# Eight broadcast copies issued behind the first RWKV spill of the second block instead of in the first block

## The chip, the cores and the metric

The kernel runs on one core of a Trainium2 chip. The metric is the device time of one execution in microseconds (us). A profiled execution gives a trace with a time for each instruction of the five engines: TensorE (PE; PEld is its weight load), VectorE (DVE), ScalarE (ACT), GpSimd (POOL) and SyncE (SP), which here only issues DMAs.

## The reference

One inference step of a layer of a diffusion backbone, over 256 context and 2,048 latent tokens (64 columns wide), width 1,024. Cut to what matters:

```
h      = rmsnorm(x) * (1 + scale) + shift          # modulation from c and c_ctx
u      = h @ w_in                                  # one input projection
att    = 8 heads: latent tokens attend 8 x 16 neighbours and all context keys,
         score = q k / 8 + rpb[head, row offset, column offset]
rwkv   = 8 heads of RWKV-7 in two directions: kr, r, v (after a width-3 convolution),
         decay and a from two loras, then a scan over the tokens
x      = x + gate * (concat(att, rwkv) @ w_out)
x      = x + gate * ffn(modulated rmsnorm(x))      # gated, width-3 convolution
```

`rpb` holds the learned offsets of the neighbourhood attention. The attention stage reads them from a table in DRAM, `d_rep`, in which each head's 23 rows of 128 values stand 16 times.

## The kernel before, in words

The stages run one after the other: `stage_in` (0 to about 1,180 us), the neighbourhood attention, the scan, the output projection, the FFN. The change lies in `stage_in` (L538).

*Column tiles.* The input projection is worked in 3 blocks `b` of 768 tokens. For each block, 12 tiles of 128 attention columns are computed first, b = 0, 1, 2; then `rwkv_columns` (L808) computes the RWKV columns of b = 2, 1, 0: three lora tiles and four pairs `p` of heads, each pair as three tiles `kr`, `r`, `v`. A tile is one `gemm`: 48 matmuls (L55), three passes (high and low parts of both factors) over 8 slices of the depth. Its weights are loaded two tiles ahead by DMAs that ACT issues (`Weights`, L79) and split by ACT and POOL (L36, L46). The modulated input `h` of block 0 is made in place and spilled to `d_hhi` (SP, L615) and `d_hlo` (ACT, L616); the other blocks load it back.

*Side work of the attention tiles.* `background(f)` runs after each of the 36 attention tiles and takes steps from the generators in the list `side`: `modulate` twice (8 steps and a first one that loads `x` by DMAs on ACT, computes its scale on ACT, L125 and L126, and scales it on DVE, L577; the transposes are L595), then one entry that calls `replicate`, then `rwkv_constants` (its transpose is L771) and `ada_rest` (the other modulation columns; transposes L240, sums L232). Two steps are taken if two or three entries are left, or if one is left and f is even; one step otherwise.

*The copies.* `replicate` (L737) issues eight DMAs on SP (L741). Each writes `d_rep[h]`, 23 x 16 x 128 values, from `rpb[h]` by a broadcast. They are held by `issue_after(W.last.ins)`, where `W.last` is the newest weight load, an instruction of ACT.

*Work behind the RWKV tiles.* `rest(b, p)` is a generator that turns `kr`, `r`, `v` of a pair into the scan's inputs; it is stepped inside the matmuls of the next pair's tiles (8 times a tile). It computes `kk` (L844), the two gates, transposes `v` and spills it to `d_v` (SP, L864), and then for each direction n = 0, 1 writes `ar` (DVE L897 and POOL L898) and `bk` (DVE L893, L896) and stores both (SP, L900). `ar` and `bk` have one buffer each. The results of a tile leave PSUM through `conv3` (ACT L114, DVE L116).

*Order.* Instructions of an engine run in its own order; a scheduler makes these orders from the program's text and dependences when the kernel is built. DMAs of SP and ACT signal through a common set of eight completion semaphores (DMAHW0 to DMAHW7), and a DMA waits until the last one with the same semaphore is done.

Of the kernel before, what the change touches and what calls it, by code (L numbers as in the profile page):

```python
# [33 lines left out]
def copy(eng, dst, src, scale=None):  # L34
    if hasattr(eng, "activation"):
        eng.activation(dst, src, AF.Copy, scale=1.0 if scale is None else scale)  # L36
    elif scale is None:
        eng.tensor_copy(dst, src)
    else:
        eng.tensor_scalar_mul(dst, src, scale)  # L40
# [8 lines left out]
def gemm3(nc, ps, halves, w, h, tick=None):  # L49


    for c in range(KT):
        for n, (A, B) in enumerate(((w[0], h[0]), (w[1], h[0]), (w[0], h[1]))):
            for q, (a, e) in enumerate(halves):
                nc.tensor.matmul(  # L55
                    ps[q][:, : e - a], A[:, c, :], B[c][:, a:e], start=c == 0 and n == 0, stop=c == KT - 1 and n == 2
                )
        if tick:
            tick()
# [61 lines left out]
def rms_scale(nc, pool, x, eps, name):  # L121

    junk = pool.tile([128, D], F32, name=name + "j", tag="rmsj", bufs=1)
    s = pool.tile([128, 2], F32, name=name + "s", tag="rmss", bufs=4)
    nc.scalar.activation(junk, x, AF.Square, accum_out=s[:, 0:1])  # L125
    nc.scalar.activation(s[:, 1:2], s[:, 0:1], AF.Sqrt, bias=eps, scale=1.0 / D)  # L126
    nc.vector.reciprocal(s[:, 0:1], s[:, 1:2])
    return s[:, 0:1]
# [17 lines left out]
def xrows(xp, xs, t):  # L146

    return xp[t * 128 : t * 128 + 128, :] if t < 2 else xs[(t - 2) * 128 : (t - 1) * 128, :]
# [384 lines left out]
def pair_cols(base, p):  # L533

    return ((base + p * 64, 64), (base + 256 + p * 64, 64))


def stage_in(tc, keep, ident, eps, I, P, C, d, R, new_k, new_v):  # L538

    nc = tc.nc  # L540
    wv = I["w_in"][0].rearrange("(c p) f -> p c f", p=128)
    hv = [d[n].rearrange("(c p) n -> p c n", p=128) for n in ("hhi", "hlo")]
    tiles = [((f * 128, 128),) for f in range(12)] * 3
    for b in range(3):
        tiles += [((3072 + i * 128, 128),) for i in range(3)]
        for p in range(4):
            tiles += [pair_cols(1536 + o, p) for o in (512, 0, 1024)]
    with tc.tile_pool(name="k1", bufs=1) as k1, tc.tile_pool(name="g2", bufs=2) as gp, tc.tile_pool(
        name="gps", bufs=2, space=PSUM
    ) as gps:  # L550

        def window(b, cols=(0, WIN)):
            h = [[], []]
            for c in range(KT):
                for x in range(2):
                    t = gp.tile([128, WIN], F32R, name=f"h{x}", bufs=9)
                    if cols:
                        a, e = cols
                        nc.scalar.dma_start(t[:, a:e].bitcast(F32), hv[x][:, c, STARTS[b] + a : STARTS[b] + e])
                    h[x].append(t)  # L560
            return h

        def gemm(h, halves, tick=None):
            ps = [gps.tile([128, 512], F32, name=f"g{q}") for q in range(2)]
            gemm3(nc, ps, halves, W.next(), h, tick)
            W.fetch()
            return ps

        with tc.tile_pool(name="q2", bufs=2) as q2, tc.tile_pool(name="qp", bufs=3, space=PSUM) as qp:
            def load(tiles):  # L570

                out = []
                for j, t in enumerate(tiles):
                    x = q2.tile([128, D], F32, name="x", bufs=8)
                    nc.scalar.dma_start(x, xrows(I["x_prompt"][0], I["x_sample"][0], t))
                    r = rms_scale(nc, q2, x, eps, f"r{j}")
                    nc.vector.tensor_scalar_mul(x, x, r)  # L577
                    out.append(x)
                return out

            def modulate(groups, h=None):


                xs = [load(g) for g in groups]
                yield
                i = 0
                for c in range(KT):
                    rows = slice(c * 128, c * 128 + 128)
                    for g, x in zip(groups, xs):
                        n = len(g) * 128  # L590
                        tok = slice(g[0] * 128, g[0] * 128 + n)
                        m = int(g[0] >= 2)
                        p = qp.tile([128, 512], F32, name="mtp")[:, :n]
                        for j, t in enumerate(x):
                            nc.tensor.transpose(p[:, j * 128 : j * 128 + 128], t[:, rows], ident)  # L595
                        t = q2.tile([128, n], F32, name="mt", tag="zz", bufs=9)
                        if h:
                            hi, lo = h[0][c][:, tok], h[1][c][:, tok]
                        else:
                            hi = q2.tile([128, n], F32R, name="mhi", tag="zz", bufs=9)  # L600
                            lo = q2.tile([128, n], F32R, name="mlo", tag="zz", bufs=9)
                        mc, ac = mul[:, m, c : c + 1], add[:, m, c : c + 1]
                        if i % 3 == 2:
                            nc.vector.tensor_scalar(t, p, mc, ac, op0=ALU.mult, op1=ALU.add)
                            copy(nc.scalar, hi, t)
                        else:
                            nc.scalar.activation(t, p, AF.Identity, scale=mc, bias=ac)
                            copy(nc.vector, hi, t)
                        (nc.vector if h or i % 3 == 0 else nc.gpsimd).tensor_sub(lo, t, hi)
                        i += 1  # L610
                        if not h:
                            nc.sync.dma_start(d["hhi"][rows, tok], hi.bitcast(F32))
                            nc.scalar.dma_start(d["hlo"][rows, tok], lo.bitcast(F32))
                    if h:
                        nc.sync.dma_start(d["hhi"][rows, 0:BLK], h[0][c][:, :BLK].bitcast(F32))  # L615
                        nc.scalar.dma_start(d["hlo"][rows, 0:BLK], h[1][c][:, :BLK].bitcast(F32))  # L616
                    yield

            h = window(0, None)
            first = modulate(GROUPS[:2], h)  # L620
            cond, ones, mul, add = ada_first(
                tc, keep, gp, q2, qp, ident, I["c"][0], I["c_ctx"], I["w_ada"][0], I["b_ada"][0], I["norm1"][0]
            )
            for _ in first:
                pass
            W = Weights(nc, gp, wv, tiles)
            side = [modulate(GROUPS[2:4]), modulate(GROUPS[4:])]
            consts = {}
            side.append(iter(lambda: replicate(tc, C["rpb"], d["rep"], W) or "end", "end"))
            side.append(rwkv_constants(tc, k1, q2, qp, ident, P, consts, W))  # L630
            side.append(ada_rest(tc, q2, qp, cond, ones, I["w_ada"][0], I["b_ada"][0], d["rows"], W))

            def background(f):
                for _ in range(2 if len(side) in (2, 3) or len(side) == 1 and f % 2 == 0 else 1):
                    if side and next(side[0], "end") == "end":
                        side.pop(0)

            for b in range(3):
                if b:
                    h = window(b, ((1, 1 + BLK), (0, WIN))[b - 1])  # L640
                for f in range(12):
                    attention_columns(nc, q2, qp, ident, gemm(h, ((b, b + 384), (b + 384, b + 768))), b, f, d, new_k, new_v)
                    background(f)
            while side:
                background(0)
        rwkv_columns(tc, ident, consts, R, h, window, gemm)


def query_parts(b):
# [84 lines left out]
        tp_out(z, new_v)  # L734


def replicate(tc, rpb, rep, W):  # L737

    with tc.issue_after(W.last.ins):
        for h in range(8):  # L740
            tc.nc.sync.dma_start(rep[h], rpb[h][:, None, :].to_broadcast([23, 16, 128]))  # L741

# [62 lines left out]
    out.update(col=col, wts=wts, lw=lw, bones=bones, tiny=tiny, cmask=cmask)  # L805


def rwkv_columns(tc, ident, consts, R, h, window, gemm):  # L808


    nc = tc.nc
    with tc.tile_pool(name="i1", bufs=1) as i1, tc.tile_pool(name="i2", bufs=2) as i2, tc.tile_pool(
# [15 lines left out]
        def rest(b, p, kr, r, v, lora):  # L828
# [29 lines left out]
            for t in range(0, 6, 3):  # L858
# [2 lines left out]
                    nc.tensor.transpose(tp[:, j * 128 : j * 128 + 128], v[:, (t + j) * 128 : (t + j) * 128 + 128], ident)  # L861
                nc.scalar.activation(vt[:, t : t + 3, :], tp[:, :384].rearrange("p (t d) -> p t d", t=3), AF.Copy)
                yield
            nc.sync.dma_start(  # L864
                R["v"].rearrange("(t p) f -> p t f", p=128)[:, b * 6 : b * 6 + 6, p * 128 : p * 128 + 128], vt
            )
            ms = []
            for n in range(2):
                sg, a = lr[2 * n : 2 * n + 2]
# [68 lines left out]
        for b in (2, 1, 0):  # L938
            if b < 2:
                h = window(b)  # L940
# [633 lines left out]
```

## Time and profile before

| | |
|---|---|
| device time, median of 3 runs | 4527.84 us (4527.21 to 4528.01) |
| the profiled execution: device time | 4528.56 us |
| its span from first to last instruction | 4526.8 us |
| granted TensorE clock, mean over the span | 0.932 of full speed (2.4 GHz) |
| PE / DVE / POOL / ACT busy, share of the span | 85% / 69% / 51% / 41% |
| `d_rep` copies | 8, issued between 30.4 and 122.1 us |
| first read of `d_rep` | 1213.5 us |

Times below are counted from the start of the span. A row of a timeline gives start, duration, engine, line of the kernel, what is written and read, and, in brackets, how long the engine stood idle before it and what ended that. "SPq" and "ACTq" are DMA issues on these engines; the duration there is the issue alone or, for several in one row, to the end of the last.

### The profile page before, as it was taken

To read this page: it belongs to the slowest core of one execution; us is meant where nothing else is said; L and a number is where in the kernel's file an instruction comes from. 1 tells how busy PE (TensorE), PEld (TensorE's weight loads), DVE (VectorE), ACT (ScalarE), POOL (GpSimd) and SP (SyncE) were. 2 spreads that over 40 slices of the span, in tenths; PEclk is the share of its full clock that TensorE was granted. 3 is DMA by queue.
4 is the path that set the end of the run, shared out by engine and by line. 5 is a ranking of instruction groups with operands and counts; after the bars stand their busy time and mean duration, and the time that the engine had idled before them with its cause. 6 is when DMAs were issued, how large, how long until landed. Compare 5 with 4: busy or idle time off the path is not lost. (4 is left out here: it accounts for less than half of the span.)

```text
span 4526.8 us, 78134 instructions
## 1 busy us (share of the span) xinstructions
PE 3852.0 (85%) x29954; PEld 3414.9 (75%) x29954; DVE 3115.0 (69%) x4658; ACT 1845.9 (41%) x3728; POOL 2323.6 (51%) x1879
## 2 busy tenths in 40 slices
PE   6798987888388887899886886999988999889996
PEld 6787877777266666788775665888877999779995
DVE  4325586868577774566664224888888888878887
ACT  2421254544377773455442223333334333343332
POOL 0334344545234336555664444666656776667662
PEclk9899998989599997999998997999988999999998
DMA  5787545453756623323343443221223222232222
GB/s 211 243 280 212 145 117 165 114 159 112 178 116 135 128 58 102 86 76 81 95 102 105 167 149 94 61 66 61 66 80 112 68 64 70 84 106 63 70 70 66
DMA packets 682387, 513.24 MB, mean 113 GB/s; under 512 B 234691, under 2 KB 612612, under 8 KB 677916
## 3 DMA queue, kind: packets, MB, share of 16 engines
q1 hardware_dynamic: 508444, 378.64, 30.0%
q10 hardware_dynamic: 170080, 118.06, 8.8%
q0 software_dynamic: 3488, 11.54, 0.8%
q8 instruction: 236, 3.87, 0.4%
q14 instruction: 139, 1.14, 0.1%
HBM read 369.85 MB, written 139.76 MB: 113 GB/s over the span
## 5 line engine op out<-in xcount | busy, mean ns | idle before, releaser
L46 POOL TENSOR_TENSOR wl<-wr,wh 128x512 fp32r<-128x512 f32 (+1 forms) x349 | 613.2, 1758 | 575.3 <-ACT wh L36 503.8
L55 PE MATMUL g<-h,wh 128*128 128x384 f32 (+1 forms) x2592 | 641.8, 359 | 32.3 <-DVE r L116 8.4
L36 ACT ACTIVATE wh<-wr 128x512 fp32r<-128x512 f32 (+1 forms) x485 | 336.3, 704 | 500.2 <-DMA wr<-in_w_ffn_dram 210.1
L55 PEld LDWEIGHTS g<-h,wh 128*128 128x128 f32 x2592 | 487.6, 200 | 67.1 <-issue 27.7
L507 DVE TENSOR_TENSOR yacc<-yacc,yp 128x512 f32<-128x512 f32 x756 | 479.3, 680 | 28.9 <-PE yp L499 5.2
L456 PE MATMUL u<-hT,wh 128*128 128x386 f32 x1056 | 366.8, 347 | 38.3 <-DVE st L465 24.8
L456 PE MATMUL u<-lT,wh 128*128 128x386 f32 x1056 | 364.4, 345 | 12.2 <-DVE lT L46 12.2
L456 PE MATMUL u<-hT,wl 128*128 128x386 f32 x1056 | 364.4, 345 | 3.8 <-POOL wl L46 3.8
L55 PE MATMUL g<-h,wl 128*128 128x384 f32 (+1 forms) x1296 | 359.9, 355 | 0.0
L499 PE MATMUL yp<-w2h,gh 128*128 128x512 f32 x792 | 273.1, 418 | 48.6 <-DVE yacc L507 20.0
L46 DVE TENSOR_TENSOR wl<-wr,wh 128x512 fp32r<-128x512 f32 (+1 forms) x136 | 251.9, 1853 | 63.2 <-ACT wh L36 63.1
L456 PE MATMUL u<-h,wh 128*128 128x386 f32 x792 | 272.7, 344 | 19.3 <-ACT h L36 17.5
L456 PE MATMUL u<-l,wh 128*128 128x386 f32 x792 | 271.7, 345 | 8.2 <-DVE l L46 7.9
L456 PE MATMUL u<-h,wl 128*128 128x386 f32 x792 | 274.4, 346 | 0.0
L499 PE MATMUL yp<-w2l,gh 128*128 128x512 f32 x792 | 257.8, 404 | 0.0
L499 PE MATMUL yp<-w2h,gl 128*128 128x512 f32 x792 | 257.0, 403 | 0.0
L55 PEld LDWEIGHTS g<-h,wl 128*128 128x128 f32 x1296 | 250.8, 200 | 2.8 <-issue 2.5
L456 PEld LDWEIGHTS u<-hT,wh 128*128 128x128 f32 x1056 | 203.0, 192 | 51.8 <-DVE st L465 31.9
L499 PEld LDWEIGHTS yp<-w2h,gh 128*128 128x128 f32 x792 | 151.6, 193 | 108.9 <-DVE yacc L507 50.1
L354 POOL TENSOR_TENSOR s<-wr 128x512 f32<-128x512 f32 x66 | 85.8, 1300 | 271.3 <-DMA wr<-in_w_ffn_dram 271.3
L456 PEld LDWEIGHTS u<-lT,wh 128*128 128x128 f32 x1056 | 203.4, 193 | 17.8 <-DVE lT L46 17.5
L1273 DVE TENSOR_TENSOR X<-iv,mmask 128x256 f16<-128x256 f32 x360 | 146.3, 422 | 98.7 <-PE iv L1270 93.8
(333 smaller groups left out, 10085.3 us busy)
## 6 DMA issues: line engine op xcount, KB each, us to landing
wr<-in_w_ffn_dram SPq DMA_DIRECT2D x198, 512.0 KB
wr<-in_w_in_dram ACTq DMA_DIRECT2D x45, 512.0 KB
wr<-in_w_in_dram ACTq DMA_DIRECT2D x72, 256.0 KB
d_ar<-ar SPq DMA_DIRECT2D x24, 768.0 KB
d_bk<-bk SPq DMA_DIRECT2D x24, 768.0 KB
kd<-d_ks SPq DMA_DIRECT2D x32, 576.0 KB
bk<-d_bk SPq DMA_DIRECT2D x72, 256.0 KB
ar<-d_ar SPq DMA_DIRECT2D x288, 64.0 KB
```

The lines of the kernel that those rows point to most:

```text
L36: eng.activation(dst, src, AF.Copy, scale=1.0 if scale is None else scale)
L46: lo_eng.tensor_sub(lo, src, hi)
L55: nc.tensor.matmul(ps[q][:, : e - a], A[:, c, :], B[c][:, a:e], start=c == 0 and n == 0, stop=c == KT - 1 and n == 2)
L354: nc.gpsimd.tensor_sub(s3, a11, a21)
L456: nc.tensor.matmul(acc[q], A[a][x][:, c, :], T[t][c][y], start=i < 3 and c == 0 and n == 0, stop=c == KH - 1 and n == 2, skip_group_check= ...
L499: nc.tensor.matmul(yps[q], A[:, t * 128 : t * 128 + 128], B[:, q * 512 : q * 512 + 512], start=n == 0, stop=n == 2)
L507: nc.vector.tensor_add(d, d, yps[q])
L1273: nc.vector.tensor_mul(half(X1, n), X, mk)
```

## The change

`replicate` is no longer an entry of `side`. It is handed to `rwkv_columns`, which calls it once, in `rest`, behind the `d_v` spill of block b=1, pair p=0, and `issue_after` now names that spill. `side` thus begins with four entries, not five.

```diff
@@ stage_in
             consts = {}
-            side.append(iter(lambda: replicate(tc, C["rpb"], d["rep"], W) or "end", "end"))
             side.append(rwkv_constants(tc, k1, q2, qp, ident, P, consts, W))
...
-        rwkv_columns(tc, ident, consts, R, h, window, gemm)
+        rwkv_columns(tc, ident, consts, R, h, window, gemm, lambda at: replicate(tc, C["rpb"], d["rep"], at))
@@ replicate
-def replicate(tc, rpb, rep, W):
+def replicate(tc, rpb, rep, at):
-    with tc.issue_after(W.last.ins):
+    with tc.issue_after(at.ins):
         for h in range(8):
             tc.nc.sync.dma_start(rep[h], rpb[h][:, None, :].to_broadcast([23, 16, 128]))
@@ rwkv_columns, rest
-            nc.sync.dma_start(
+            at = nc.sync.dma_start(
                 R["v"].rearrange("(t p) f -> p t f", p=128)[:, b * 6 : b * 6 + 6, p * 128 : p * 128 + 128], vt
             )
+            if b == 1 and p == 0:
+                behind(at)
```

SP's queue at the start, before (`wb`, `wa` are the modulation's weights, `h_...` the slices of the first block's `h`):

```order
L176 DMA wb<-in_w_ada_dram 128x1024
L741 DMA d_rep<-in_rpb_dram 368x1x128 x3
L615 DMA d_hhi<-h_98 128x768
L615 DMA d_hhi<-h_100 128x768
L741 DMA d_rep<-in_rpb_dram 368x1x128
L615 DMA d_hhi<-h_102 128x768
L615 DMA d_hhi<-h_104 128x768
L741 DMA d_rep<-in_rpb_dram 368x1x128
L615 DMA d_hhi<-h_106 128x768
L615 DMA d_hhi<-h_108 128x768
```

The same place after the change:

```order
L176 DMA wb<-in_w_ada_dram 128x1024
L237 DMA arow<-in_b_ada_dram 1x512
L615 DMA d_hhi<-h_98 128x768
L615 DMA d_hhi<-h_100 128x768
L615 DMA d_hhi<-h_102 128x768
L615 DMA d_hhi<-h_104 128x768
L615 DMA d_hhi<-h_106 128x768
L615 DMA d_hhi<-h_108 128x768
```

The copies are gone from between the spills, and one load of `ada_rest` has come to the front.

SP's queue in `rest` of b=1, p=0, after the change (before, `d_ar` followed the `d_v` spill directly; lines of the changed kernel, one to three off those before):

```order
L901 DMA d_bk<-bk 128x12x128
L863 DMA d_v<-vt 128x6x128
L740 DMA d_rep<-in_rpb_dram 368x1x128 x8
L901 DMA d_ar<-ar 128x12x128
L901 DMA d_bk<-bk 128x12x128
L922 DMA d_g_73<-m_6369 64x768
L901 DMA d_ar<-ar 128x12x128
```

All eight copies stand in a row between that pair's `d_v` spill and its first store of `ar`.

DVE between the two writes of `ar` of that pair, before: n=0 is the first row, n=1 the last.

```order
L897 TENSOR_TENSOR ar<-kk,e_4084 128x12x64
L883 SCALAR_TENSOR_TENSOR t_6314<-zones,w_6210 128x768
L876 TENSOR_TENSOR sl<-m_6282,m_6284 128x768
L877 TENSOR_TENSOR sq<-sq,sl 128x768
L893 SCALAR_TENSOR_TENSOR bk<-a_6234,e_6317 128x12x64
L896 TENSOR_TENSOR bk<-t_6324,e_6317 128x12x64
L116 SCALAR_TENSOR_TENSOR r<-g_6201,cols,r 128x386
L116 SCALAR_TENSOR_TENSOR r<-g_6202,cols,r 128x382
L897 TENSOR_TENSOR ar<-kk,e_4085 128x12x64
```

After the change, the end of that stretch:

```order
L116 SCALAR_TENSOR_TENSOR kr<-g_6446,cols,kr 128x384
L854 TENSOR_SCALAR w_6553<-w_6553 128x768
L854 TENSOR_SCALAR a_6577<-a_6577 128x768
L898 TENSOR_TENSOR ar<-kk,e_4077 128x12x64
L843 SCALAR_TENSOR_TENSOR kk<-kr,cols,sq 128x768
L875 SCALAR_TENSOR_TENSOR sq<-r,cols,kr 128x768
L116 SCALAR_TENSOR_TENSOR r<-g_6544,cols,r 128x386
```

The write for n=1 (`e_4077`) now stands 27 rows behind that for n=0, just ahead of the next pair's `kk` and of the evacuation of `r` of the third pair.

## Rows read from the trace of the kernel before

**Rows 1.** Part 1 of the page: for each engine busy us, its share of the span, and the number of instructions, over the whole span.
```profile
PE 3852.0 (85%) x29954; PEld 3414.9 (75%) x29954; DVE 3115.0 (69%) x4658; ACT 1845.9 (41%) x3728; POOL 2323.6 (51%) x1879
```

**Rows 2.** The table by stretches of time: from:to in us, the stretch's length, then busy us of PE, PEld, DVE, ACT and POOL (xinstructions), the granted TensorE clock, the share of the DMA engines and GB/s.
```profile
40.00:80.00 40.00, 31.93 (x157) 28.59 (x157) 18.58 (x41) 9.89 (x17) 5.21 (x2) 0.99 0.37 131
80.00:120.00 40.00, 19.77 (x77) 18.57 (x77) 5.42 (x8) 5.82 (x13) 1.80 (x1) 0.71 0.43 146
120.00:160.00 40.00, 28.14 (x141) 26.60 (x142) 17.57 (x23) 17.20 (x35) 20.49 (x12) 0.80 0.74 224
160.00:200.00 40.00, 38.88 (x232) 37.52 (x231) 12.69 (x22) 16.98 (x37) 15.81 (x10) 0.99 0.91 279
850.00:900.00 50.00, 42.11 (x208) 37.16 (x207) 40.78 (x36) 25.49 (x38) 28.05 (x14) 0.93 0.45 132
```

**Rows 3.** The instructions that write or read the offset rows `d_rep` (times in the issuing queue: min/median/max ns, first to last start in us).
```profile
L1086 SPq DMA_DIRECT2D raw<-d_rep x64: 302/303/1035, 1213.5 to 1617.2; - x64
L741 SPq DMA_DIRECT2D d_rep<-in_rpb_dram x8: 626/656/10110, 30.4 to 122.1; - x8
```

**Rows 4.** The DMA view of the stretch 44 to 50 us (the packets and rate in it, and what was issued in it), in which only copies of `d_rep` are in flight.
```profile
DMA packets 256, 0.13 MB, mean 22 GB/s; under 512 B 1, under 2 KB 256, under 8 KB 256
...
d_rep<-in_rpb_dram SPq DMA_DIRECT2D x1, 184.0 KB
```

**Rows 5.** Timeline of the SP queue at the start: start us, duration, line, what is issued, count (an entry with a count above 1 runs to the end of its last).
```profile
30.36 19.80 SPq L741 DMA_DIRECT2D d_rep<-in_rpb_dram  x3
...
62.91 14.31 SPq L615 DMA_DIRECT2D d_hhi<-h  x2
...
91.06 15.60 SPq L615 DMA_DIRECT2D d_hhi<-h  x1
```

**Rows 6.** Timeline of ACT in the same stretch; in brackets the idle time before the instruction and what ended it.
```profile
66.91 0.42 ACT L36 ACTIVATE h<-mt 128x256 fp32r<-128x256 f32 x1 [5.63 <-DMA d_rep<-in_rpb_dram]
...
92.84 0.94 ACT L688 ACTIVATE zq<-g 128x256 f32<-128x256 f32 x3 [9.47 <-DMA d_rep<-in_rpb_dram]
...
120.52 0.29 ACT L126 ACTIVATE r2s<-r2s,eps 128x1 f32<-128x1 f32 x1 [18.68 <-DMA d_qs<-zh]
```

**Rows 7.** Timeline of PE, 82 to 141 us: start, duration, line, out<-in, shapes, count, and in brackets the idle time before it and what ended it.
```profile
82.85 1.01 PE L55 MATMUL g<-h,wh 128*128 128x384 f32 x2 [7.52 <-DVE h L38]
...
85.25 1.48 PE L55 MATMUL g<-h,wh 128*128 128x384 f32 x4
...
89.08 0.87 PE L55 MATMUL g<-h,wh 128*128 128x384 f32 x4
...
93.45 0.83 PE L55 MATMUL g<-h,wh 128*128 128x384 f32 x2 [2.80 <-ACT zq L688]
...
96.86 0.48 PE L595 MATMUL mtp<-ident,x 128*128 128x128 f32 x1 [2.41 <-DVE x L577]
...
121.85 0.48 PE L595 MATMUL mtp<-ident,x 128*128 128x128 f32 x1 [14.03 <-DVE x L577]
123.22 1.12 PE L595 MATMUL mtp<-ident,x 128*128 128x128 f32 x4 [0.89 <-DVE x L577]
127.25 0.47 PE L595 MATMUL mtp<-ident,x 128*128 128x128 f32 x1 [2.91 <-DVE x L577]
...
140.48 0.90 PE L595 MATMUL mtp<-ident,x 128*128 128x128 f32 x3 [2.47 <-DVE mt L604]
```

**Rows 8.** Waits of PE from 128 to 560 us: line, what it waited for, us in all, times, longest.
```profile
PE mtp L240 <- DVE acc L232: 12.9, 6, 3.5
PE aux L771 <- DMA h<-d_hlo: 10.3, 1, 10.3
...
PE g L55 <- DMA h<-d_hlo: 3.2, 2, 2.4
```

**Rows 9.** Timeline of the SP queue in the second block (b=1) of the RWKV columns.
```profile
807.11 0.36 SPq L864 DMA_DIRECT2D d_v<-vt  x1
807.58 0.48 SPq L900 DMA_DIRECT2D d_ar<-ar  x1
...
859.25 0.37 SPq L900 DMA_DIRECT2D d_ar<-ar  x1
```

**Rows 10.** Timeline of ACT there: the first and the last of eight weight loads that ACT issues between these two times (814.02, 819.48, 822.23, 829.93, 840.07, 846.41, 851.12 and 865.67).
```profile
814.02 0.38 ACTq L79 DMA_DIRECT2D wr<-in_w_in_dram  x1
...
865.67 0.37 ACTq L79 DMA_DIRECT2D wr<-in_w_in_dram  x1
```

**Rows 11.** Part 6 of the page (DMA issues): what, queue, count, KB each.
```profile
wr<-in_w_in_dram ACTq DMA_DIRECT2D x72, 256.0 KB
d_ar<-ar SPq DMA_DIRECT2D x24, 768.0 KB
```

**Rows 12.** Timeline of DVE there.
```profile
847.91 0.53 DVE L855 TENSOR_SCALAR a<-a 128x768 f32<-128x768 f32 x1
...
861.63 1.64 DVE L116 SCALAR_TENSOR_TENSOR r<-g,cols,r 128x386 f32<-128x386 f32 x3
863.57 2.90 DVE L897 TENSOR_TENSOR ar<-kk,e 128x768 f32<-128x768 f32 x1 [0.30 <-DMA d_ar<-ar]
```

**Rows 13.** Timeline of PE there.
```profile
863.32 0.44 PE L55 MATMUL g<-h,wh 128*128 128x386 f32 x1 [0.76 <-DVE r L116]
869.02 1.01 PE L823 MATMUL lr<-sl,bones 128*128 128x384 f32 x2 [5.26 <-DVE sl L46]
```

More of the change, by code (lines that the diff above doesn't have):

```diff
@@ L805, in rwkv_constants, with rwkv_columns @@
     out.update(col=col, wts=wts, lw=lw, bones=bones, tiny=tiny, cmask=cmask)
-def rwkv_columns(tc, ident, consts, R, h, window, gemm):
+def rwkv_columns(tc, ident, consts, R, h, window, gemm, behind):
     nc = tc.nc
```

## The prediction

> **What bounds the kernel now.** First the share of each engine: TensorE (PE) is busy 85% of the span [rows 1], so an idle stretch of PE is what a change can remove or add. Then the table by stretches [rows 2]: PE works 31.93 of 40 us from 40 to 80, but only 19.77 from 80 to 120 and 28.14 from 120 to 160, with the granted clock at 0.71 and 0.80, and 38.88 from 160 to 200 at 0.99. So the start has a hole. Third, who owns that hole: the copies `d_rep` are issued there, between 30.4 and 122.1 us, though the first reader (L1086) comes at 1213.5 [rows 3]. Fourth, what such a copy costs: with only these in flight, 256 packets of 512 B pass in 6 us, 22 GB/s [rows 4], so 23.4 ns a packet. A copy of 184 KB is 368 packets, 8.6 us; eight are 69 us, one after another even when three are queued.
>
> **How they stop PE now.** SP's queue stands at the spills of `h` for 14.31 and 15.60 us with a copy in between [rows 5]. ACT, which issues DMAs as well and in order, stands still 5.63 and 9.47 us for a copy and 18.68 us for a transfer queued among them [rows 6]. ACT also issues the loads of `x` and computes their scale, so PE waits for `x`: [rows 7] give, between 82.85 and 127.25, waits of 7.52, 2.80, 2.41, 14.03, 0.89 and 2.91, together 30.6 us.
>
> **The change, part by part.**
>
> *Start.* The eight copies leave the head of SP's queue; nothing takes their place but one `arow` load, which comes earlier. The 30.6 us go. With them goes the slow clock after each long wait: four matmuls take 1.48 us at 85.25 but 0.87 at 89.08, when PE has been at work again for 6 us [rows 7]: 0.15 us each. Between 82.85 and 89.08 some 19 matmuls fit at that pace, and as many follow the waits at 93.45 and 96.86: 5 us. What is late next is the modulation chain itself, which is at work when no copy is in the way: one wait like that at 140.48, 2.47 us [rows 7]. Gain 30.6 + 5 − 2.5 = **33 us**. Its ends: if only ACT's and `h`'s waits go and the four waits for `x` stay (2.41 + 14.03 + 0.89 + 2.91 = 20.2), 13 us; if nothing replaces the waits, 36 us. I take 33, because the waits for `x` end with ACT instructions that themselves stood behind the copies [rows 6].
>
> *Pacing of the side work.* The list `side` has four entries in place of five, so the rule "two steps when two or three are left" sets in one entry earlier: the last group of modulations runs two steps a tile instead of one, constants and the `ada` columns come some five to eight tiles earlier. No work is added. PE's waits around it now are 12.9 us for `ada`, 10.3 us at the constants' transpose and 3.2 us for `h` at a block's start [rows 8]. All the `ada` waits gone would be −13; another wait like that of the constants +10. Modulation's spills come in about half the time while the DMA engines are already at 0.91 [rows 2]; I charge one more set of `h` waits, **+3 us**.
>
> *New place.* All eight copies now stand in SP's queue right behind the `d_v` spill of the second block's first pair, issued at T = 807.11 [rows 9]. Nobody waits for them. But the next thing on SP is the store of `ar` for n=0, ready at 807.58 [rows 9]. `ar` has one buffer, so DVE's and POOL's writes of `ar` for n=1 wait for that store to land. Its share on the engine that the copies occupy lies behind all of them. When does it land? About 2 us until the first copy moves; 69 us of copies; weight loads that ACT issues meanwhile, 8 of them [rows 10] of 256 KB [rows 11], which is 1,024 pieces of 256 B, 64 to an engine if spread over 16: 512 packets at between half of and the full 23.4 ns, 6 to 12 us, taken as 9; and the store itself, 4.3 us from its issue at 859.25 [rows 9] to the write that it releases at 863.57 [rows 12]. T + 84, or 891.
>
> DVE works in order. The changed order puts 27 rows of DVE between its two writes of `ar`; the last of them ran before at 847.91 [rows 12], so DVE stops only near T + 41. Behind that write stand the next pair's `kk`, a product, and the evacuation of `r` of the third pair (L116), which before ran at 861.63 [rows 12]. PE's next column tile needs that PSUM buffer: it started at 863.32, T + 56 [rows 13]. After the change: T + 84, then 2.9 us for the write [rows 12], about 2 for `kk` and the product, 1.64 for the evacuation [rows 12]: T + 90.5. PE loses 34 us. A little of PE's other waits there (5.26 at 869.02 [rows 13]) may fall inside; but DVE is busy 40.78 of 50 us in this stretch [rows 2], so its backlog keeps PE from catching up. **+33 us.** Ends: if the store passes the copies and only ACT's semaphores hold (ACT's load of 865.67, T + 58.6 [rows 10], waits for the last copy, T + 71), about +12; if the weight loads take full packet times and PE also gives up the slow clock after a long wait, 34 + 3 + 5 = +42.
>
> A rule to weigh here: the Trainium skill, "DMA: Bandwidth & Descriptors", section "Specifications", gives about 27 GiB/s an engine. An estimate from that page: 188,416 B take 6.5 us, eight 52 us, the new stall is 17 us shorter and the sum is −14 in place of +3. The trace has 22 GB/s and 8.6 us, and the measurement decides.
>
> *Everything later* (attention, scan, output, FFN) keeps its order on every engine; `d_rep` is ready at about T + 80 = 890, 320 us ahead of its reader [rows 3]. Cost 0; cover is that distance.
>
> **Sum.** −33 + 3 + 33 = +3 us on the profiled 4528.56, 4531.6; the runs' median, 4527.84, lies 0.7 lower: **4531 us**. About 0.2% (9 us) is what a measurement of this kernel can tell from no change; +3 is inside it.
>
> **The rivals.**
>
> *A. The copies are hidden at the new place (chance 0.16).* If they ran beside the `ar` store on other engines, or DVE had enough other work, only −33 + 3 is left: 4498 us, faster. For it: PE's work there is not DMA-bound (share 0.45 [rows 2]). Against it: the 22 GB/s of [rows 4] with three queued, and the single `ar` buffer. With only the +12 end: 4510, also faster. The Trainium skill, "DMA: Bandwidth & Descriptors", section "Why a DMA increments its semaphore by 16 and not by 1", speaks against A: a DMA runs on the largest number up to 16 that divides the slowest dimension of both sides, on the lowest-numbered engines; 23 and 368 leave one engine, the same for all eight. By that rule, with which 22 GB/s in [rows 4] agrees, A would need the store to skip that engine.
>
> *B. The waits for `x` stay (chance 0.2).* The start is bound by the loads of `x` and the scale of them, whatever SP does: 20.2 us of the 33 are not won, and the new place costs in full: 4531 + 20 = 4551, slower. It decides as soon as more than 6 us of those 20.2 stay (3 + 6 is over 9). For it: ACT's wait that is the longest, 18.68, is put down to `d_qs`, not to a copy [rows 6]. Against it: that transfer was issued among the copies, and ACT's turn waits on completions shared with SP.
>
> *C. The new pacing decides (chance 0.1).* Crowded spills delay the second block's `h` or the constants by another 10.3 [rows 8]: 4542; or the `ada` waits go: 4515.
>
> **How the numbers follow.** The forecast, with its sizes a little off either way, has 0.54; within it some seven tenths fall inside 0.2% (0.39), 0.11 above and 0.04 below, since the late stall can grow by 9 and the start gain by 3 only. A 0.16 (faster), B 0.2 (slower), C 0.1 (split). Faster 0.25, same 0.39, slower 0.36. The likeliest case alone runs from 4518 to 4543. The range, 4508 to 4554, takes in B, C, and A's partly hidden end of 4510; left out are A's full gain and a late stall at its upper end together with B.
>
> **What would show it.** In the profile after: (1) no `d_rep` before 800; PE's waits for `x` near 100 to 127 gone, PE over 34 of 40 us from 80 to 120, granted clock above 0.9; PE's work of 127.25 done near 95. (2) One run of eight copies from about 775 (T moves by the gain), and 70 to 85 us at some 22 GB/s. (3) The first `ar` write that waits on `DMA d_ar` with 35 to 45 us idle on DVE, and PE idle about 34 us before a column tile, released by DVE `r`. (4) Past it, spans equal to before. I am wrong if (3) shows less than 20 us, or (1) leaves more than 6 us of waits for `x`.

## The result: slower by a third of a percent

| | before | after |
|---|---|---|
| median of 6 runs | 4527.52 us | 4542.85 us (4535.17 to 4546.35) |
| ratio, with 95% interval | | 1.0033 (1.002 to 1.0047) |
| the profiled execution | 4528.56 us, span 4526.8 | 4537.57 us, span 4535.8 |

The change costs 15 us by the medians (9 between the two profiled executions, of which the one after is among the fastest). That is outside the 0.2% that the prediction called no change, and inside its range of 4508 to 4554.

**The hole at the start is gone.** The table by stretches of the changed kernel answers [rows 2] (columns as there):

```profile
40.00:80.00 40.00, 37.04 (x193) 34.35 (x194) 23.05 (x47) 14.58 (x27) 7.07 (x3) 1.00 0.58 216
80.00:120.00 40.00, 33.75 (x186) 32.51 (x186) 19.03 (x25) 18.45 (x38) 21.19 (x12) 0.94 0.82 251
120.00:160.00 40.00, 39.92 (x236) 38.51 (x235) 12.68 (x22) 18.06 (x41) 15.75 (x11) 0.98 0.90 282
850.00:900.00 50.00, 22.13 (x93) 19.59 (x94) 34.59 (x31) 18.05 (x25) 25.70 (x11) 0.67 0.60 174
```

PE works 37.04, 33.75 and 39.92 us where it worked 31.93, 19.77 and 28.14, and the clock of 80 to 120 us is 0.94 in place of 0.71. A new hole stands at 850 to 900: 22.13 us of 50, against 42.11. The copies stand in one row ahead of it, from 778.6 us on, and the first reader comes 7.3 us later than in [rows 3]:

```profile
L1087 SPq DMA_DIRECT2D raw<-d_rep x64: 302/303/1242, 1220.8 to 1626.3; - x64
L740 SPq DMA_DIRECT2D d_rep<-in_rpb_dram x8: 733/9166/10417, 778.6 to 837.2; - x8
```

Of the waits for `x` that [rows 7] show, one is left in PE's timeline between 60 and 135 us:

```profile
89.92 0.33 PE L595 MATMUL mtp<-ident,x 128*128 128x128 f32 x1 [2.26 <-DVE x L577]
```

**How much was won, and how much was lost on the way to the new place.** Two stretches of equal work, cut at the starts of the 1st, 11th and 42nd column tile (a tile is 48 matmuls of L55); first the kernel before, then the changed one:

```profile
56.40:204.80 148.40, 110.08 (x574) 104.79 (x575) 48.09 (x80) 47.95 (x101) 39.12 (x23) 0.86 0.67 213
204.80:551.00 346.20, 309.26 (x1643) 284.18 (x1642) 164.43 (x245) 91.62 (x166) 125.61 (x57) 0.96 0.73 223
```

```profile
56.20:163.40 107.20, 100.85 (x575) 97.68 (x575) 48.62 (x80) 48.16 (x101) 39.23 (x23) 0.97 0.88 285
163.40:521.70 358.30, 316.79 (x1643) 284.79 (x1642) 173.84 (x245) 92.29 (x166) 118.75 (x57) 0.95 0.69 215
```

The first stretch takes 107.2 us in place of 148.4, 41.2 less: PE's time without work falls from 38.3 to 6.4 us (32), and the same 574 or 575 matmuls are busy 9.2 us less, at a clock of 0.97 in place of 0.86. The second stretch takes 358.3 in place of 346.2, **12.1 more**: 4.6 more without work, 7.5 more busy time for the same 1643 matmuls at a slightly lower clock (0.95, before 0.96). So more than half of what the new pace costs is not a wait but longer busy time. PE's waits there, against [rows 8]:

```profile
PE mtp L240 <- DVE acc L232: 9.9, 5, 5.1
PE aux L722 <- ACT zh L718: 6.8, 4, 3.4
PE g L55 <- DMA h<-d_hlo: 4.9, 4, 1.9
PE g L55 <- DMA h<-d_hhi: 3.9, 4, 1.5
PE g L55 <- DVE zl L694: 3.6, 2, 2.4
PE aux L770 <- DMA zh<-in_w_ts_dram: 3.5, 1, 3.5
```

The constants' wait shrank from 10.3 to 3.5 and that for the `ada` sums from 12.9 to 9.9, but `h` (4.9 and 3.9, before 3.2 and 1.9), the attention columns' high and low parts (5.8, before 1.0) and the parts that the transposes of L722 read (9.6, before 7.5) are waited for more.

**The new place.** SP's queue of the changed kernel, which answers [rows 9]; T is the `d_v` spill's issue:

```profile
778.15 0.37 SPq L863 DMA_DIRECT2D d_v<-vt  x1
778.57 67.18 SPq L740 DMA_DIRECT2D d_rep<-in_rpb_dram  x8
845.86 8.49 SPq L901 DMA_DIRECT2D d_ar<-ar  x1
```

T comes 29.0 us earlier than before (807.11). The eight copies hold SP for 67.18 us, and the store of `ar` behind them, ready at T, is issued only at 845.86; its own issue takes 8.49 us, where it took 0.48. DVE, ACT, POOL and PE, in this order (against [rows 12, 13]):

```profile
816.48 0.63 DVE L854 TENSOR_SCALAR a<-a 128x768 f32<-128x768 f32 x1 [3.40 <-ACT a L852]
859.73 0.96 DVE L898 TENSOR_TENSOR ar<-kk,e 128x768 f32<-128x768 f32 x1 [42.62 <-DMA d_ar<-ar]
860.72 2.31 DVE L843 SCALAR_TENSOR_TENSOR kk<-kr,cols,sq 128x768 f32<-128x768 f32 x1
...
864.00 2.18 DVE L116 SCALAR_TENSOR_TENSOR r<-g,cols,r 128x386 f32<-128x386 f32 x4
```

```profile
862.25 1.05 ACT L114 ACTIVATE r<-g,cols 128x385 f32<-128x385 f32 x2 [42.55 <-POOL ar L899]
```

```profile
859.84 2.38 POOL L899 TENSOR_TENSOR ar<-r,e 128x768 f32<-128x768 f32 x1 [43.15 <-DMA d_ar<-ar]
```

```profile
865.80 1.18 PE L55 MATMUL g<-h,wh 128*128 128x386 f32 x2 [36.36 <-DVE r L116]
...
881.75 0.69 PE L822 MATMUL lr<-sh,bones 128*128 128x384 f32 x1 [9.85 <-ACT sh L36]
...
886.26 1.01 PE L822 MATMUL lr<-sl,bones 128*128 128x384 f32 x2 [2.22 <-DVE sl L46]
```

The store lands at about 859.7, T + 81.6. DVE stood 42.62 us before its second write of `ar`, POOL 43.15, and ACT 42.55 behind POOL's half of `ar`: POOL reads `r` of the first pair there, and the third pair's evacuation on ACT (L114) takes that buffer. PE waits 36.36 us for that evacuation, and 9.85 and 2.22 more for the backlog. From the 61st to the 65th column tile's start the changed kernel falls back by 38.7 us (from 29.6 ahead to 9.1 behind); before, then changed:

```profile
824.70:884.90 60.20, 52.04 (x254) 44.82 (x252) 48.19 (x42) 31.45 (x46) 25.66 (x12) 0.94 0.44 124
```

```profile
795.10:894.00 98.90, 50.48 (x243) 44.54 (x242) 44.58 (x41) 26.73 (x39) 28.30 (x13) 0.74 0.38 106
```

PE's time without work rises from 8.2 to 48.4 us; its busy time doesn't grow.

### The profile page after: what moved, and what is told of

The parts are those of the page before. It is cut to its first block, busy times and chain, and to the rows that moved or that the text cites. A ratio compares the mean times of both kernels' runs of the same rounds, so it can differ in the third digit from the quotient of the medians.

```text
span 4535.8 us, 78126 instructions
## 1 busy us (share of the span) xinstructions
PE 3848.6 (85%) x29954; PEld 3405.7 (75%) x29954; DVE 3124.3 (69%) x4658; ACT 1847.0 (41%) x3728; POOL 2317.3 (51%) x1879
## 5 line engine op out<-in xcount | busy, mean ns | idle before, releaser
L55 PE MATMUL g<-h,wh 128*128 128x384 f32 (+1 forms) x2592 | 638.1, 357 | 66.4 <-DVE r L116 42.8
L55 PEld LDWEIGHTS g<-h,wh 128*128 128x128 f32 x2592 | 484.7, 199 | 104.8 <-issue 65.9
L507 DVE TENSOR_TENSOR yacc<-yacc,yp 128x512 f32<-128x512 f32 x756 | 479.5, 680 | 29.9 <-PE yp L499 6.3
L456 PE MATMUL u<-lT,wh 128*128 128x386 f32 x1056 | 364.0, 345 | 14.4 <-DVE lT L46 14.3
L55 PE MATMUL g<-h,wl 128*128 128x384 f32 (+1 forms) x1296 | 359.1, 355 | 0.0
L55 PEld LDWEIGHTS g<-h,wl 128*128 128x128 f32 x1296 | 250.0, 200 | 2.2 <-issue 1.9
```

The costliest lines, as they stand in the source:

```text
L55: nc.tensor.matmul(ps[q][:, : e - a], A[:, c, :], B[c][:, a:e], start=c == 0 and n == 0, stop=c == KT - 1 and n == 2)
L456: nc.tensor.matmul(acc[q], A[a][x][:, c, :], T[t][c][y], start=i < 3 and c == 0 and n == 0, stop=c == KH - 1 and n == 2, skip_group_check= ...
L507: nc.vector.tensor_add(d, d, yps[q])
```

## The experiments

Each is one kernel, timed beside the kernel before on the same chip, with 4 to 12 runs; the kernel before had medians from 4526.31 to 4527.52 in these timings. The first columns are the median and the ratio to the kernel before with its 95% interval. The last two are read from rows on `d_rep` in each profiled execution: the first copy's issue where the copies stand at the new place (start and pace together; a place 807.5 in the kernel before would be the same), and the first read of `d_rep`, which ends the stage (1213.5 before).

| kernel | median us | ratio | first copy | first read |
|---|---|---|---|---|
| the change | 4542.85 | 1.0033 (1.0020 to 1.0047) | 778.6 | 1220.8 |
| e1: new place, old pace | 4527.98 | 1.0003 (0.9993 to 1.0013) | 763.3 | 1208.3 |
| e2: old place, new pace | 4550.78 | 1.0053 (1.0037 to 1.0068) | | 1228.5 |
| e3: new place, wide copies | 4506.36 | 0.9951 (0.9937 to 0.9965) | 781.8 | 1189.6 |
| e4: old place, wide copies | 4491.79 | 0.9919 (0.9904 to 0.9935) | | 1169.6 |
| e5: new place, wide, old pace | 4490.97 | 0.9916 (0.9903 to 0.9930) | 765.8 | 1174.5 |
| e6: the change, two `ar` buffers | 4536.09 | 1.0021 (1.0012 to 1.0030) | 784.1 | 1220.6 |
| e7: POOL issues the copies | 4506.06 | 0.9951 (0.9938 to 0.9965) | | 1188.3 |
| e8: one copy per spill, old pace | 4482.43 | 0.9905 (0.9891 to 0.9918) | 761.7 | 1161.8 |
| e9: e5, modulations early | 4488.40 | 0.9914 (0.9900 to 0.9927) | 762.0 | 1168.9 |
| e10: e9, constants early too | 4497.89 | 0.9936 (0.9924 to 0.9949) | 775.9 | 1186.0 |
| e11: e8 with wide copies | 4473.46 | 0.9885 (0.9873 to 0.9898) | 762.0 | 1152.7 |
| e12: e8 with e9's pace | 4485.39 | 0.9906 (0.9893 to 0.9919) | 767.2 | 1167.5 |

### e1: the new place with the old pace

```diff
+            side.append(iter(()))
             side.append(rwkv_constants(tc, k1, q2, qp, ident, P, consts, W))
```

> The copies at the new place, but `side` begins with five entries again (an empty one in the place of the copies' entry), so the side work runs at the old pace. Theory (three separate terms: start -41, pacing +13, late stall +41): the pacing term goes, the late stall stays; about 4529 us, 0.2 to 0.4% below the change (4542), PE's wait of some 36 us near 865 still there, and the tiles from the 11th to the 42nd take about 347 us, not 360. Rival (the pace as such costs nothing; the 13 us are the price of everything starting 41 us earlier): 4542, and those tiles still take about 360.

Measured 4527.98: no difference to the kernel before. The late stall is unchanged, in PE's timeline and in the row on the copies:

```profile
850.13 1.19 PE L55 MATMUL g<-h,wh 128*128 128x386 f32 x2 [35.78 <-DVE r L116]
```

```profile
L741 SPq DMA_DIRECT2D d_rep<-in_rpb_dram x8: 733/9205/10412, 763.3 to 821.5; - x8
```

The stretch from the 11th to the 42nd column tile:

```profile
163.70:506.00 342.30, 308.36 (x1643) 282.64 (x1643) 164.94 (x245) 91.69 (x166) 120.49 (x57) 0.97 0.74 225
```

The first copy comes 44.2 us earlier than the place in the kernel before, 15.3 earlier than in the change. The stretch takes 342.3 us, 16.0 less than in the change (7.6 of it without work, 8.4 busy). So the new pace alone costs 15 to 16 us in this setting, the start is worth a little over 40, and the late stall takes that back. The rival falls.

### e2: the old place with the new pace

```diff
-            side.append(iter(lambda: replicate(tc, C["rpb"], d["rep"], W) or "end", "end"))
+            replicate(tc, C["rpb"], d["rep"], W)
```

> The reverse: the copies are called before the attention tiles, outside `side`, so they stand at the head of SP's queue as before, and `side` begins with four entries. Theory of three separate terms: 4527.5 + 13 = about 4540, the hole from 75 to 127 us as before, no late stall, the tiles from the 11th to the 42nd 360 us. Rival (the pace as such costs nothing): 4528, 347 us.

Measured 4550.78, more than either forecast: from the 11th to the 42nd tile's start the kernel takes 14.4 us more than before, and the scheduler put two copies side by side at the start (SP issues them from 105.69 us in 12.05 us), where the hole grew: the 11th tile starts 5.2 us later than before. PE's longest wait for `x` there, 14.03 in [rows 7]:

```profile
131.88 1.11 PE L595 MATMUL mtp<-ident,x 128*128 128x128 f32 x4 [19.59 <-DVE x L577]
```

The new pace costs its 12 to 16 us with the copies at either place; the rival (the pace as such costs nothing) is out here too.

### e3 and e4: the copies spread over the DMA engines

```diff
-            tc.nc.sync.dma_start(rep[h], rpb[h][:, None, :].to_broadcast([23, 16, 128]))
+            tc.nc.sync.dma_start(rep[h].rearrange("r x c -> x r c"), rpb[h][None].to_broadcast([16, 23, 128]))
```

> As the change, but each copy is written with the 16 repeats as the outermost dimension (16 x 23 x 128 on both sides, same bytes to the same addresses). Theory (the late stall is a DMA engine that works alone): the copy spreads over the engines, 23 packets each, some 0.6 us of work; issue of all eight takes 6 to 8 us in place of 67, PE's wait of 36 us falls under 5, total 4542 - 40 = about 4503 (4497 to 4510). Rival (what counts is that eight issues stand ahead of the store, or the bytes, not the engine): a stall of over 20 us stays, 4525 to 4542.

> As the kernel before, copies at the start and old pace, but written with the 16 repeats outermost. Theory (the hole from 75 to 127 us is the one busy DMA engine): the hole goes though the copies stay in the same places, 4527.5 - 38 = about 4489 (4485 to 4495). Rival B of the prediction (PE waits for `x` whatever the copies do): at most half of it goes, 4508 or more. Second rival (it is the place in SP's queue ahead of the spills that hurts): 4520 or more.

The same bytes go to the same addresses; only the order of the dimensions differs. e3 takes 4506.36, e4 4491.79, both within what the first theory gave (e4 in its range, e3 in its). The row on the copies and PE's next column tile in e3:

```profile
L740 SPq DMA_DIRECT2D d_rep<-in_rpb_dram x8: 550/618/779, 781.8 to 796.1; - x8
```

```profile
839.43 1.19 PE L55 MATMUL g<-h,wh 128*128 128x386 f32 x2 [6.70 <-DVE r L116]
```

An issue takes 0.62 us in place of 9.2, all eight are out by 796.7, 15 us after the first in place of 67 (6 to 8 expected), and PE's wait falls from 36.36 to 6.70 us (under 5 expected). In e4, with the copies among the first spills as before, the stretches of [rows 2] read:

```profile
L741 SPq DMA_DIRECT2D d_rep<-in_rpb_dram x8: 557/593/762, 30.3 to 85.9; - x8
```

```profile
40.00:80.00 40.00, 37.04 (x197) 34.38 (x198) 23.04 (x47) 14.04 (x26) 7.07 (x3) 1.00 0.65 229
80.00:120.00 40.00, 32.87 (x179) 31.78 (x178) 19.40 (x25) 19.16 (x40) 21.66 (x12) 0.91 0.81 247
```

The hole is gone with the copies still there. How many DMA engines SP's queue (q1) keeps at work while only copies were issued on it, first in the change from 821 to 845 us, then in e3 from 782 to 787 (packets, MB, and the time that they took as a share of 16 engines):

```profile
q1 hardware_dynamic: 961, 0.49, 6.7%
```

```profile
q1 hardware_dynamic: 2368, 1.17, 80.5%
```

The narrow copies keep 6.7% busy, about one engine of sixteen (6.25%), the wide ones 80.5%. So at the old place it was neither the place nor the bytes, but the one engine that the copies ran on, and at the new place nearly all of it. The rule from the Trainium skill, "DMA: Bandwidth & Descriptors", section "Why a DMA increments its semaphore by 16 and not by 1", says that the slowest dimension decides the number of engines. The two shares, for 23 and for 16 outermost, agree with it.

### e5: old pace and wide copies at the new place

> New place, old pace, copies written with the 16 repeats outermost. If start, pacing and late stall add up: start and pace -45 (as the run with the old pace showed at the 42nd tile), late stall +5 (as the wide run showed), so 4527.4 - 40 = about 4487, level with or 5 below the wide copies at the old place (4492). If they don't add up (the wide run's 4506 is bound by something that the earlier start meets), it stays at 4500 or more.

Measured 4490.97, 35 us below the kernel before, where the sum of terms gave 40. The terms add up to within 5 us, and e5 is level with e4 (the intervals overlap): where wide copies stand makes no difference that these runs can tell.

### e6: two buffers for `ar`

```diff
-                ar = i2.tile([128, 12, 2, 64], F32, name="ar", bufs=1)
+                ar = i2.tile([128, 12, 2, 64], F32, name="ar", bufs=2)
```

> As the change, with two buffers for `ar` in place of one. If the single buffer is what turns the late store into a stall (the prediction's reading), the wait of DVE shrinks to under 10 us and the time to about 4510. If SP's queue itself stands for 67 us, the next pair's write of `ar`, which takes the buffer of the store that is not even issued, waits for the same moment: DVE's wait moves one instruction group down and stays above 30 us, 4535 to 4542. I expect the second.

Measured 4536.09, 7 us below the change. DVE's wait and PE's:

```profile
865.05 0.96 DVE L898 TENSOR_TENSOR ar<-kk,e 128x768 f32<-128x768 f32 x1 [37.17 <-DMA d_ar<-ar]
```

```profile
867.73 1.18 PE L55 MATMUL g<-h,wh 128*128 128x386 f32 x2 [28.99 <-DVE r L116]
...
882.75 0.69 PE L822 MATMUL lr<-sh,bones 128*128 128x384 f32 x1 [8.26 <-ACT sh L36]
```

As expected, the wait moved to the next pair's write of `ar`: 37.17 us on DVE and 28.99 + 8.26 on PE. The prediction named the single buffer as the reason; from the 61st to the 65th tile's start the second one takes 10 us off the 38.7, and SP's 67 us are the rest. By the medians it is 7 us, with intervals that overlap; in its trace e6 came to this stretch 9 us later than the change did, so that both end the stage level (first read 1220.6 and 1220.8).

### e7: another queue

```diff
-            tc.nc.sync.dma_start(rep[h], rpb[h][:, None, :].to_broadcast([23, 16, 128]))
+            tc.nc.gpsimd.dma_start(rep[h], rpb[h][:, None, :].to_broadcast([23, 16, 128]))
```

On the old pace. Here nothing holds the copies at the new place, since `issue_after` names an instruction of SP.

> Old pace, the copies as the change writes them (23 rows outermost), but issued by POOL; POOL's order puts them at its head, so they go out in the first microseconds. Theory (SP's and ACT's own issues stand still behind a slow copy in the queue): with another queue SP and ACT issue freely and share at most one DMA engine; the hole from 75 to 127 us and the late stall both go, about 4490 plus what the first loads lose (0 to 20): 4490 to 4510. Rival (the busy engine alone holds every transfer that has a share on it, whatever the queue): the first 70 us are stretched, 4520 or more.

Measured 4506.06, inside the first forecast. The copies' rows and two stretches of the start:

```profile
L741 POOL DMA_DIRECT2D d_rep<-in_rpb_dram x8: 2360/2389/2727, 1.4 to 67.9; - x8
...
DMA to landing us min/median/max: 11.7/14.2/34.8
```

```profile
40.00:60.00 20.00, 17.62 (x83) 17.27 (x83) 9.02 (x20) 4.78 (x9) 6.32 (x3) 1.00 0.37 108
60.00:80.00 20.00, 9.24 (x33) 7.11 (x34) 9.32 (x15) 2.74 (x6) 9.44 (x4) 1.00 0.40 106
```

Between 60 and 80 us PE works 9.24 us of 20. The first column tile starts at 75.2 us, in e5 at 56.3: until 60 us PE waits 16.2 us in all for the modulation's weights `wb` (5.1 in e5), whose last load SP issues at 39.0 in place of 29.9. By the eighth column tile's start 17.9 us are won where e5 wins 40.6; at the last column tile 13 of that distance are left. The issuer matters (SP is not held for 67 us, and there is no late stall), and the first transfers are slowed all the same. POOL's DMAs run on a queue of another kind (`software_dynamic` in the page, those of SP and ACT `hardware_dynamic`), and which engines they used is not shown, so this run alone does not part the queue from the engine.

### e8: one copy per spill

```diff
-            if b == 1 and p == 0:
-                behind(at)
+            if b < 2:
+                behind(at, (1 - b) * 4 + p)        # issues the copy of this one head
```

Old pace, narrow copies.

> Old pace, narrow copies, but one behind each of the eight `d_v` spills of blocks 1 and 0 in place of eight behind one. Theory (the stall comes when SP's issue of the next `ar` store is pushed past the slack of that store, and 67 us are far past it): one copy delays it by 9 us; the write for n=1 stood 10 us behind the store's issue, so 0 to 4 us a pair: 4527.4 - 45 + (0 to 30), 4483 to 4513. Rival (the total time of the copies on their engine counts, wherever they stand): 4528 as with all eight in one place.

Measured 4482.43, at the low end of the first forecast, 46 us below e1 with the same copies, bytes and pace. SP's queue at the first of them:

```profile
761.73 0.74 SPq L740 DMA_DIRECT2D d_rep<-in_rpb_dram  x1
762.58 8.10 SPq L901 DMA_DIRECT2D d_ar<-ar  x1
770.77 2.62 SPq L901 DMA_DIRECT2D d_bk<-bk  x1
```

The store of `ar` still takes 8.10 us to issue behind a copy, and `d_bk` 2.62; but the next write of `ar` comes late enough to wait only 0.82 us for it on DVE, and PE does not wait there. Behind the third copy it is a store of `bk` that is held, and PE feels it (SP, DVE, PE):

```profile
855.17 10.61 SPq L901 DMA_DIRECT2D d_bk<-bk  x1
```

```profile
873.00 0.96 DVE L894 SCALAR_TENSOR_TENSOR bk<-a,e 128x768 f32<-128x768 f32 x1 [8.36 <-DMA d_bk<-bk]
```

```profile
875.41 1.32 PE L822 MATMUL lr<-lora,l_w 64*128 64x384 f32 x3 [4.82 <-DVE m L918]
```

One copy of 8 us mostly hides, eight in a row don't. The rival falls.

### e9 and e10: which part of the new pace costs

Both are e5 with `len(side) in (2, 3, 4)` in the rule, and with an entry of ten empty steps in `side`; the list in short:

```
e9:  side = [modulate, modulate, range(10), rwkv_constants, ada_rest]
e10: side = [modulate, modulate, rwkv_constants, range(10), ada_rest]
```

> As the wide copies at the new place with the old pace, but the last group of modulations runs two steps a tile (as in the change) and then ten empty steps follow, so that the constants and the `ada` columns come where they came before. It tells which half of the new pace costs its 13 to 17 us. Theory 1 (crowded modulation: spills and POOL's work in half the time): nearly all of it, 4487 + 13 = 4500. Theory 2 (`ada` and constants under the second block's load of `h` and `q`, `k` transposes): little, 4487 + 0 to 4. The tile times gave -41 to -34 during the crowded modulation and -34 to -20 in the six tiles behind it, so I expect a third: 4492.

> Wide copies at the new place; the last modulations and the constants come as early as in the change, then ten empty steps, so that only the `ada` columns stay where they were. With the run that held back both (4488) it tells whether the constants or the `ada` columns cost the new pace its 15 us. If early `ada` columns do (their loads, DVE sums and transposes fall into the second block's tiles): about 4488. If the constants do: 4500 to 4506.

By the first copy's issue: e5 765.8, modulations early 762.0, constants early too 775.9, `ada` columns early too (e3) 781.8. The medians say the same: 4490.97, 4488.40, 4497.89, 4506.36. The crowded modulations, which the prediction charged with 3 us, cost nothing in the end; the early constants cost about 10 to 14 us and the early `ada` columns 6 to 8 (the intervals of e10 and e3 overlap, so this second size rests on the traces). I had expected a third in e9, and of e10 one or the other: it is both. From the 11th to the 42nd column tile, e9 and e10:

```profile
164.90:506.50 341.60, 306.45 (x1643) 280.24 (x1643) 170.39 (x245) 91.75 (x167) 113.66 (x57) 0.98 0.74 225
```

```profile
164.00:518.30 354.30, 313.81 (x1643) 285.78 (x1642) 163.55 (x245) 92.18 (x166) 120.20 (x57) 0.96 0.71 217
```

Of the 12.7 us that early constants add, 5.3 are waits and 7.4 are busy time of the same 1643 matmuls, at a clock of 0.96 in place of 0.98. Through which of the many short waits that comes is left open.

### e11 and e12: the best version

e11 is e8 with the wide copies, e12 is e8 with e9's pace.

> One copy behind each of the eight spills, old pace, and each written with the 16 repeats outermost. With eight narrow ones spread so the time was 4482.4 and PE had no added wait there. If SP's 8 us hold per pair cost nothing, this is the same, 4480 to 4485; if they cost 0.5 us a pair, 4478.

> One narrow copy per spill, last modulations at two steps a tile, ten empty steps, constants and `ada` columns where they were. At the 42nd tile the early modulations had won 2 to 3 us over the old pace: 4482.4 - 2 = about 4480, within the interval of the one without them; if it is the best of all by over 4 us, the early `h` of the next block is worth more than the tile times showed.

e11 takes **4473.46 us, 0.9885 of the kernel before** (0.9873 to 0.9898), 54 us less, and 9 below e8, more than I expected:

```profile
762.04 0.66 SPq L740 DMA_DIRECT2D d_rep<-in_rpb_dram  x1
762.80 0.71 SPq L901 DMA_DIRECT2D d_ar<-ar  x1
```

The store is issued in 0.71 us, the stage is level with e8 at the first copy (762.0 and 761.7) and ends 9.1 us earlier (1152.7 and 1161.8): SP's 8 us a pair did cost, though not evenly. About 5 of the 9 us lie at the held store of `bk` shown under e8, which e11 issues in 0.36 us. The intervals of e8 and e11 touch (0.9891 to 0.9898), so the size rests on these two traces. e12, 4485.39, is no better than e8 (the two intervals overlap), so e9's 2.6 us over e5 don't carry over and are not to be counted on.

## Why the prediction was right in two terms and wrong in the third

- *Start.* Forecast −33, measured −41.2. The mechanism held: waits fell by 32.0 us. Too small was the slow clock: I counted 5 us, it was 9.2, because it lasted to the end of the hole (0.71 and 0.80 in [rows 2]), not only after its first waits; and the 2.5 us that I left for the modulation chain stood in the kernel before as well, so they were no loss. Rival B is out: 2.26 us of waits for `x` are left of 20.2. One sign was just missed: PE works 33.75 of 40 us from 80 to 120, where I had named over 34.
- *Pacing.* Forecast +3, measured +12.1 in the change, 16.0 against e1, 14.4 in e2. This is the step that failed. I took one set of `h` waits as the price, and looked for it at the modulations' spills. e9 shows these at no cost; constants and `ada` columns, moved into the second block's attention tiles, cost 9 and 8 us by the medians (e10, e3), and more than half of it is busy time at a lower clock (7.5 of the 12.1 us, 7.4 of 12.7 in e10), which a sum of waits cannot show. Rival C's 4542 is the measured time, but not by its way: it had `h` or the constants wait another 10.3 us, where the constants' wait fell to 3.5.
- *New place.* Forecast +33 (12 to 42), measured +38.7: PE waited 36.36 where I had 34, but I let the backlog vanish in PE's other waits, and it cost 9.85 and 2.22 more. The moment was right (T + 81.6, forecast T + 84), the way to it was not: I had the store issued early and its packets queued behind the copies. In the trace SP itself stands, and the store goes out only at T + 67.7; either way it comes behind all eight copies, so the moment is the same. That difference matters for a remedy: a second buffer takes only 10 us off (e6). ACT was not held by semaphores but by a buffer that POOL still read.
- *Sum.* −41.2 + 12.1 + 38.7 = +9.6, forecast +3; the last column tile starts 9.3 us later than before, the profiled executions differ by 9.0, the medians by 15. Two terms of about equal size cancelled as forecast, and the small third one decided the sign. That their errors, 8 us more won and 6 more lost, nearly cancelled too is luck.
- *Rival A* (the copies hide) is false for eight narrow copies in a row. It is nearly true for wide ones (e5, with a wait of 6.70 us left as in e3) and for narrow ones spread out (e8).
- *The page's figure.* An estimate from the 27 GiB/s an engine in the Trainium skill, "DMA: Bandwidth & Descriptors", section "Specifications", was 6.5 us a copy, and the sum by it had the wrong sign. SP's 67.18 us for eight (8.4 each) and the 22 GB/s of [rows 4] agree with each other and not with it.

## What to carry to other kernels

A transfer that nobody waits for is not free: ask how many DMA engines it runs on and what stands behind it in its queue, and move or reshape it only after that. Here reshaping alone, which needs no new place, was worth 36 us, and one copy per spill 44; eight in one row gave back all that the start had won. And when an entry leaves a list that paces other work, cost the new pace as a change of its own, in busy time at the granted clock as well as in waits.

## What the runs showed of the hardware that I had not expected

- In these traces the issue of a DMA itself took about as long as the slow one ahead of it in the same queue: `ar`'s store took 8.49 us to issue behind a row of copies, 8.10 behind one, 0.71 behind a wide one and 0.48 before. Copies issued behind one another took 9.2 us each (median); where other work stood between them, a copy took 0.66 and the entry behind it the wait (14.31 us for two spills, [rows 5]). What holds the issue is not shown. In e11 against e8, from 760 to 1,140 us, PE is busy 286.65 us for 1,373 matmuls in place of 292.08 for 1,372, at a clock of 0.86 in place of 0.84, so over half of the 9 us between them was longer busy time.
- The order of dimensions of one copy, with the same bytes and addresses, moved the whole kernel by 36 us.
- Issued by POOL, the same narrow copies took 11.7 to 34.8 us each to land, and other transfers of the first 60 us were still slowed: PE's waits for `wb` were 16.2 us, without them there 5.1.
